# Expert passes of a two-block transformer kernel: gate tables from two-byte products with tokens innermost, 64 candidates for 256, all weight subtractions on VectorE

## Chip, cores and metric

The kernel runs on one core of a Trainium2 chip. The metric is the device time of one launch in microseconds (us); the median of three runs of the kernel before is 3660.84 us (3656.49 to 3661.97).

## What is computed

Two transformer blocks over 512 tokens, in float32. The change lies in the expert layer that ends the first block: 8 heads, each of which picks 16 of 16,384 one-neuron experts for each token through two lists of 128 keys.

```python
v1, i1 = lax.top_k(s1, PEER_TOPK)          # 16 of 128 keys, for each head and token
v2, i2 = lax.top_k(s2, PEER_TOPK)
cand = (v1[..., :, None] + v2[..., None, :]).reshape(PEER_CHUNK, PEER_HEADS, PEER_TOPK * PEER_TOPK)
sc, ci = lax.top_k(cand, PEER_TOPK)        # 16 of 256 sums
idx = (jnp.take_along_axis(i1, ci // PEER_TOPK, axis=-1) * PEER_N_KEYS
       + jnp.take_along_axis(i2, ci % PEER_TOPK, axis=-1))
g = jax.nn.softmax(sc, axis=-1)
act = jax.nn.gelu(jnp.einsum('chkd,cd->chk', peer_u[idx], hc), approximate=False) * g
return jnp.einsum('chk,chkd->cd', act, peer_v[idx])
```

## The kernel before

After attention and the state-space branch, the layer is worked in two passes over all experts, and for the first 128 tokens by gathers.

**Tokens 128 to 511, dense.** Pass 1 (`phase_p1`, with `experts_in` as its loop) takes 128 steps, one for each value of the second key. A step loads 512 KB of `peer_u`, splits it into a high part `whi` (ScalarE, L267) and the rest `wlo` (the subtraction of L268), and makes 24 matmuls of 384 columns into `pl` (lines 273 to 275: high by high, high by rest, rest by high). A Gelu writes `A`, and every second step a DMA writes `A` to memory (`adram`). The subtraction runs on VectorE (DVE in the profile) or, where `W.lo_eng` says so, on GpSimd (POOL): every second step of pass 1, about every third of pass 2.

**Gate tables.** `route(t)` works through tile t of 128 tokens on VectorE: the best 16 of each of 16 key lists (lines 1175 to 1179), 256 sums a head (L1186), the best 16 of these (lines 1193 to 1197), a softmax, and the two key numbers of each pick (lines 1216 to 1218, a compare, a product and a reduction of 2048 elements). For tiles 1 to 3 the picks are turned so that a token is a column, and for each block of 4 tokens (96 blocks in all) VectorE builds the one-hot tables `O`: for each token three instructions of 128 elements (lines 1251 to 1253), which take the token's key numbers and gate as one value per partition. Twelve matmuls of 128 columns (L1257) turn a block into its gate table in `pG`, ScalarE copies it to `G` (L1258), and after 8 blocks a DMA writes 2 MB to `gdram`.

**Tokens 0 to 127, sparse.** Once tile 0 is routed, 256 gathers by GpSimd (L1107) bring one row of `peer_u` or `peer_v` for each token and pick, 512 KB each, into a ring of 6; VectorE takes a dot product (L1116, 128 of them) or adds the row times its gate to `sacc` (L1126).

**Pass 2** (`phase_p2`) takes 128 steps over `peer_v`: `prep` multiplies `A` by its gate (L1289; for 8 steps at a time `fetch` reads back `A` and `G`), splits the product into `ahl` (lines 267, 268), and 18 matmuls of 512 columns go into six accumulators `acc`. After it come the second block's layers, which the change does not touch.

**What sets the order.** Each engine works its queue in order. The queue's order is fixed when the program is built, by a planner that replays the program on its own clock; the loop in `phase_p1` deals out routing and sparse work against a budget for each dense step (`have`, `some`), with the costs that stand behind `yield`. Buffers are rings by tag: `O` has 3, `A` 2, `Gst` (for `G` and for what is read back) 2.

Of the kernel before, what the change touches and what calls it, by code (L numbers as in the profile page):

```python
# [12 lines left out]
F32 = mybir.dt.float32  # L13
# [237 lines left out]
class Kernel:  # L251
# [809 lines left out]
    def phase_p1(self):  # L1061
        nc, pp = self.nc, self.pp

        ring = self.p0.tile([128, 4, D], F32, name="ring", tag="xres")
        more = pp.tile([128, 2, D], F32, name="ring2")
        self.ring = [ring[:, j] for j in range(4)] + [more[:, j] for j in range(2)]
        self.hs = pp.tile([128, D], F32, name="hs")
        nc.gpsimd.dma_start(out=self.hs, in_=self.hdram)
        self.iotab = pp.tile([128, 128], BF16, name="iotab")
        nc.vector.tensor_copy(self.iotab, self.iota)  # L1070
        self.query()
        first, rest, dense = self.route(0), chain(*(self.route(t) for t in range(1, TT))), self.experts_in()
        self.sparse = self.sparse_experts()

        have = 0.0
        for n, _ in enumerate(dense):
            have += 3.7
            while have > 0 and (d := next(first, None)) is not None:
                have -= d
            if have > 0:  # L1080
                self.some(1.0)
                have -= 1.15
                while have > 0 and (d := next(rest, None)) is not None:
                    have -= d
# [11 lines left out]
    def sparse_experts(self):  # L1096
# [4 lines left out]
        self.sacc = pp.tile([128, D], F32, name="sacc")  # L1101
# [17 lines left out]
        v.tensor_tensor(dots, dots, self.sgate, op=OP.mult)  # L1119
        for n in range(128, 256):  # L1120
            fetch(n + R - 1)
            r, w = self.ring[n % R], dots[:, n - 128:n - 127]
            if n == 128:
                v.tensor_scalar(self.sacc, r, w, None, op0=OP.mult)
            else:
                v.scalar_tensor_tensor(self.sacc, r, w, self.sacc, op0=OP.mult, op1=OP.add)  # L1126
            yield

    def query(self):
# [3 lines left out]
        for c in range(16):  # L1133
            if c < 3:
                q = self.q01[c]
            else:
                q = pp.tile([128, S], F32, name="qp", tag="A", bufs=2)
                nc.scalar.copy(q, next(self.xw))
# [6 lines left out]
    def experts_in(self):  # L1145
# [3 lines left out]
        for n in range(128):  # L1149
            self.W.lo_eng = nc.gpsimd if n % 2 else None  # L1150
# [5 lines left out]
            if n % 2 == 0:  # L1156
                A = pp.tile([128, 2, SD], F32, name="A", tag="A", bufs=2)
# [5 lines left out]
    def route(self, t):  # L1163
# [5 lines left out]
        io16 = self.iota[:, :16]  # L1169
        val = pp.tile([128, 16, 16], F32, name="val")  # L1170
        ix = pp.tile([128, 16, 16], U32, name="ix")
        for c in range(16):
            s = self.sall[t // 2][:, t % 2, c]
            w = pp.tile([128, 256], F32, name="w", bufs=1)
            v.max(val[:, c, :8], s)
            v.max_index(ix[:, c, :8], val[:, c, :8], s)
            v.match_replace(w[:, :128], val[:, c, :8], s, LOW)
            v.max(val[:, c, 8:], w[:, :128])
            v.max_index(ix[:, c, 8:], val[:, c, 8:], w[:, :128])
            yield 1.6  # L1180
        ixf = pp.tile([128, 8, 2, 16], BF16, name="ixf")
        v.tensor_copy(ixf.rearrange("p h i k -> p (h i) k"), ix)
        cand = pp.tile([128, 8, 16, 16], F32, name="cand", tag="cand")
        vv = val.rearrange("p (h i) k -> p h i k", i=2)
        sh = [128, 8, 16, 16]
        v.tensor_tensor(cand, vv[:, :, 0, :, None].to_broadcast(sh), vv[:, :, 1, None, :].to_broadcast(sh), op=OP.add)  # L1186
        yield 2.3
        sc = pp.tile([128, 8, 16], F32, name="sc")
        ci = pp.tile([128, 8, 16], U32, name="ci")
        for h in range(8):  # L1190
            s = cand[:, h].rearrange("p a b -> p (a b)")
            w = pp.tile([128, 256], F32, name="w", bufs=1)
# [5 lines left out]
            yield 2.3  # L1198
# [9 lines left out]
        k = pp.tile([128, 2, 8, 16], U32, name="k")  # L1208
        kf = pp.tile([128, 2, 8, 16], F32, name="kf")
        v.tensor_scalar(k[:, 0], ci, 4, None, op0=OP.logical_shift_right)  # L1210
        v.tensor_scalar(k[:, 1], ci, 15, None, op0=OP.bitwise_and)
        v.tensor_copy(kf, k)
        yield 1.5
        for i in range(2):
            eq = pp.tile([128, 8, 16, 16], BF16, name="eq", tag="cand")
            v.tensor_tensor(eq, kf[:, i, :, :, None].to_broadcast(sh), io16[:, None, None, :].to_broadcast(sh), op=OP.is_equal)
            v.tensor_tensor(eq, eq, ixf[:, :, i, None, :].to_broadcast(sh), op=OP.mult)
            v.tensor_reduce(r3[:, i], eq, axis=AX.X, op=OP.add)
            yield 5.5
# [18 lines left out]
        half = lambda x, h: x.bitcast(BF16).rearrange("p (n h) -> p n h", h=2)[:, :, h]
        v.tensor_copy(half(g3[:, 0], 1), half(T3[:, 2], 1))
        v.tensor_tensor(left, T3[:, 2], half(g3[:, 0], 1), op=OP.subtract)  # L1240
        v.tensor_copy(half(g3[:, 0], 0), half(left, 1))
        v.tensor_tensor(g3[:, 1], left, half(g3[:, 0], 0), op=OP.subtract)
        for b in range(0, 128, 4):
# [715 lines left out]
```

## Time and profile before

| | |
|---|---|
| median of 3 runs | 3660.84 us (3656.49 to 3661.97) |
| the profiled execution | 3660.37 us |
| its span | 3658.6 us |
| TensorE (PE) busy | 3309.3 us, 90% of the span |
| VectorE (DVE) busy | 2597.9 us, 71% |
| ScalarE (ACT) busy | 1325.2 us, 36% |
| GpSimd (POOL) busy | 1349.2 us, 37% |
| pass 1, first matmul of 384 columns to last gate table | about 586 to 1409 us |
| pass 2, first to last matmul into `acc` | 1438.0 to 2033.5 us |

Times in the trace count from the span's start. The shares are means over stages with different limits, so the stages are read one by one. Idle time carries the name of what ended it. "L268" is a line of the kernel; the subtractions of all weights have this one line.

### The profile page before, as it was taken

The page shows a single profiled execution, that of the slowest core. Times are in us where ns is not written, and L with a number is a line of the kernel's source. Part 1 is how long each engine was busy: PE and PEld are TensorE (multiplying, and loading weights), DVE is VectorE, ACT ScalarE, POOL GpSimd, SP SyncE. Part 2 cuts the span into 40 slices and gives each one's busy share as a digit, 9 for nine tenths or more (in the row PEclk, how much of TensorE's full clock was granted, in tenths as well). Part 3 has the DMA queues.
Part 4 walks back from the last instruction along what each step waited for, and adds up shares of the span by engine and source line. Part 5 has one row for each costly group of instructions (what it writes and reads, how often), then busy time and mean ns, then how long its engine had stood idle before and what let it go on. Part 6 is the DMA issues. An engine that isn't in the chain of part 4 may idle for free.

```text
span 3658.6 us, 47432 instructions
## 1 busy us (share of the span) xinstructions
PE 3309.3 (90%) x17407; PEld 2782.9 (76%) x17407; DVE 2597.9 (71%) x5062; ACT 1325.2 (36%) x2267; POOL 1349.2 (37%) x1284
## 2 busy tenths in 40 slices
PE   6877999889889785888999999999999999999998
PEld 5666789878777764666888887788888877888886
DVE  8999447999999998898555777455543686455533
ACT  4234433233233231223333366334431475334431
POOL 6577112662652643674122145431101245331101
PEclk9888999899989886999999999999999999999999
DMA  3222233975875866998665311322222311313322
GB/s 123 85 72 84 88 115 130 320 261 203 300 253 210 305 244 231 347 360 320 225 219 173 130 41 47 115 81 88 95 96 98 126 36 41 133 65 104 98 92 75
DMA packets 173867, 569.87 MB, mean 156 GB/s; under 512 B 18864, under 2 KB 52657, under 8 KB 167617
## 3 DMA queue, kind: packets, MB, share of 16 engines
q1 hardware_dynamic: 114576, 352.37, 28.6%
q0 software_dynamic: 40752, 157.30, 12.0%
q10 hardware_dynamic: 18304, 57.15, 4.1%
q8 instruction: 137, 2.24, 0.3%
q14 instruction: 98, 0.80, 0.1%
HBM read 503.33 MB, written 63.44 MB: 155 GB/s over the span
## 4 chain that ended last, share of the span: by engine, by line
PE 56%; DVE 28%; issue 7%; POOL 5%; DMA 2%; ACT 2%; SPq 0%; DVEq 0%; POOLq 0%; ACTq 0%
PE pl L273 7%; PE pl L274 7%; PE pl L275 7%; DVE ring L1116 4%; PE acc L274 4%; PE acc L275 4%; PE acc L273 3%; DVE wlo L268 2%; DVE O L1252 2%; PE mm L273 2%; PE mm L274 2%; PE mm L275 2%; DVE O L1253 2%; DVE O L1251 2%; DVE sacc L1126 1%
## 5 line engine op out<-in xcount | busy, mean ns | idle before, releaser
L267 ACT CAST whi<-wraw 128x1024 fp32r<-128x1024 f32 x523 | 544.7, 1047 | 950.4 <-PE pl L274 347.6
L268 DVE TENSOR_TENSOR wlo<-wraw,whi 128x1024 fp32r<-128x1024 f32 x352 | 448.0, 1273 | 522.5 <-ACT whi L267 508.3
L268 POOL TENSOR_TENSOR wlo<-wraw,whi 128x1024 fp32r<-128x1024 f32 x171 | 435.2, 2547 | 774.6 <-ACT whi L267 770.2
L275 PE MATMUL pl<-hhi,wlo 128*128 128x384 f32 (+1 forms) x1128 | 408.8, 365 | 64.3 <-POOL wlo L268 37.8
L273 PE MATMUL pl<-hhi,whi 128*128 128x384 f32 (+1 forms) x1128 | 407.9, 362 | 7.6 <-ACT whi L267 7.6
L274 PE MATMUL pl<-hlo,whi 128*128 128x384 f32 (+1 forms) x1128 | 404.6, 359 | 0.0
L274 PE MATMUL pl<-xTlo,whi 128*128 128x512 f32 x944 | 370.3, 392 | 0.0
L273 PE MATMUL pl<-xThi,whi 128*128 128x512 f32 x944 | 369.9, 392 | 0.0
L275 PE MATMUL pl<-xThi,wlo 128*128 128x512 f32 x944 | 367.4, 390 | 0.0
L274 PE MATMUL acc<-wlo,ahl 128*128 128x512 f32 x744 | 299.6, 403 | 21.6 <-DVE wlo L268 16.7
L273 PE MATMUL acc<-whi,ahl 128*128 128x512 f32 x744 | 254.7, 399 | 49.6 <-ACT ahl L267 28.8
L275 PE MATMUL acc<-whi,ahl 128*128 128x512 f32 x744 | 295.6, 400 | 0.0
L275 PEld LDWEIGHTS pl<-hhi,wlo 128*128 128x128 f32 x1128 | 225.1, 200 | 77.0 <-POOL wlo L268 41.9
L1107 POOL DMA_INDIRECT ring<-in_peer_v,sidx x128 | 180.6, 1411 | 199.1 <-DVE sacc L1126 136.1
L273 PEld LDWEIGHTS pl<-hhi,whi 128*128 128x128 f32 x1128 | 225.7, 200 | 18.9 <-ACT whi L267 10.2
L1107 POOL DMA_INDIRECT ring<-in_peer_r,sidx x128 | 169.3, 1323 | 165.4 <-DVE dots L1116 89.9
L274 PEld LDWEIGHTS pl<-hlo,whi 128*128 128x128 f32 x1128 | 225.1, 200 | 4.1
L1940 POOL TENSOR_TENSOR cv<-cv 128x512 f32<-128x512 f32 x44 | 57.1, 1297 | 430.7 <-ACT cv L1939 430.7
L273 PEld LDWEIGHTS acc<-whi,ahl 128*128 128x128 f32 x744 | 139.9, 189 | 88.5 <-ACT ahl L267 29.1
L273 PEld LDWEIGHTS pl<-xThi,whi 128*128 128x128 f32 x944 | 177.2, 188 | 39.0 <-issue 0.5
L275 PEld LDWEIGHTS pl<-xThi,wlo 128*128 128x128 f32 x944 | 177.2, 188 | 38.7 <-issue 0.5
L274 PEld LDWEIGHTS pl<-xTlo,whi 128*128 128x128 f32 x944 | 177.3, 188 | 36.7 <-issue 1.0
(698 smaller groups left out, 7937.5 us busy)
## 6 DMA issues: line engine op xcount, KB each, us to landing
wraw<-in_peer_u SPq DMA_DIRECT2D x128, 512.0 KB
wraw<-in_peer_v SPq DMA_DIRECT2D x128, 512.0 KB
wraw<-in_up SPq DMA_DIRECT2D x88, 512.0 KB
adram<-A ACTq DMA_DIRECT2D x64, 384.0 KB
A<-adram SPq DMA_DIRECT2D x16, 1536.0 KB
gdram<-G ACTq DMA_DIRECT2D x12, 2048.0 KB
G<-gdram SPq DMA_DIRECT2D x16, 1536.0 KB
wraw<-in_down SPq DMA_DIRECT2D x44, 512.0 KB
```

What stands on the lines that cost most here:

```text
L267: self.nc.scalar.copy(hi, src)
L268: (eng or self.nc.vector).tensor_tensor(lo, src, hi.bitcast(F32), op=OP.subtract)
L273: mm(out, l[0], r[0], start=start, stop=False)
L274: mm(out, l[0], r[1], start=False, stop=False)
L275: mm(out, l[1], r[0], start=False, stop=stop)
L1107: nc.gpsimd.indirect_dma_start(out=self.ring[n % R], out_offset=None, in_=src[n // 128], in_offset=bass.IndirectOffsetOnAxis(ap=self.sidx[ ...
L1116: v.tensor_tensor_reduce(r, r, self.hs, 1.0, 0.0, op0=OP.mult, op1=OP.add, accum_out=dots[:, n:n + 1])
L1126: v.scalar_tensor_tensor(self.sacc, r, w, self.sacc, op0=OP.mult, op1=OP.add)
L1251: v.tensor_scalar(O[:, 0, j], self.iotab, i1, None, op0=OP.is_equal)
L1252: v.tensor_scalar(Ow[:, j], self.iota, i2, ga, op0=OP.is_equal, op1=OP.mult)
L1253: v.tensor_scalar(O[:, 3, j], self.iotab, i2, gb, op0=OP.is_equal, op1=OP.mult)
L1940: nc.gpsimd.tensor_tensor(ts[0], ts[0], ts[1], op=OP.mult)
```

## The change

Five things are done. A block's tables `O` are built by two instructions in place of twelve: one compare of 1024 elements and one product of 1536, all in two-byte floats, with the four tokens innermost; a gate is held as three two-byte terms. Of the 256 sums only the 64 that can hold a best 16 are formed, in four pieces, and the place of a pick is worked back from its position by some small instructions; the two key numbers are picked by two-byte products and a tree of additions, ScalarE spreading the key numbers out. All subtractions of weights in both passes go to VectorE. The budget of `phase_p1` is changed. The first read-back is a method of its own, called from the end of pass 1 if routing is done. Ring sizes: `O` 2 for 3, `A` 3 for 2.

```diff
         for n, _ in enumerate(dense):
-            have += 3.7
+            have += 3.85
...
-                self.some(1.0)
-                have -= 1.15
...
+                self.some(1.1)
+                have -= 1.3
...
+            if n >= 122 and not left and not self.AG:
+                self.fetch_ag(0)
...
         for n in range(128):
-            self.W.lo_eng = nc.gpsimd if n % 2 else None
             w = self.W.next()
...
-        cand = pp.tile([128, 8, 16, 16], F32, name="cand", tag="cand")
+        cand = pp.tile([128, 8, 64], F32, name="cand", tag="sums")
...
+        for a, na, nb in ((0, 1, 16), (1, 3, 8), (4, 4, 4), (8, 8, 1)):
...
+        nc.scalar.copy(ei[:, 1], ix.rearrange("p (h i) k -> p h i k", i=2)[:, :, 0, :, None].to_broadcast([128, 8, 16, 16]))
...
-            eq = pp.tile([128, 8, 16, 16], BF16, name="eq", tag="cand")
-            v.tensor_tensor(eq, kf[:, i, :, :, None].to_broadcast(sh), io16[:, None, None, :].to_broadcast(sh), op=OP.is_equal)
-            v.tensor_tensor(eq, eq, ixf[:, :, i, None, :].to_broadcast(sh), op=OP.mult)
-            v.tensor_reduce(r3[:, i], eq, axis=AX.X, op=OP.add)
...
+            v.tensor_tensor(e, self.iota16[:, None].to_broadcast(sh), kb[:, i, :, None, :].to_broadcast(sh), op=OP.is_equal)
+            v.tensor_tensor(e, e, ei[:, 1], op=OP.mult)
...
+            for m in (8, 4, 2):
+                v.tensor_tensor(e[:, :, :m], e[:, :, :m], e[:, :, m:2 * m], op=OP.add)
+            v.tensor_tensor(r3[:, i], e[:, :, 0], e[:, :, 1], op=OP.add)
...
-            O = pp.tile([128, 4, 4, 128], BF16, name="O", tag="O", bufs=3)
-            Ow = O[:, 1:3].rearrange("p e j i -> p (e j i)").bitcast(F32).rearrange("p (j i) -> p j i", j=4)
-            for j in range(4):
-                i1, i2, ga, gb = (x[:, b + j:b + j + 1] for x in (T3[:, 0], T3[:, 1], g3[:, 0], g3[:, 1]))
-                v.tensor_scalar(O[:, 0, j], self.iotab, i1, None, op0=OP.is_equal)
-                v.tensor_scalar(Ow[:, j], self.iota, i2, ga, op0=OP.is_equal, op1=OP.mult)
-                v.tensor_scalar(O[:, 3, j], self.iotab, i2, gb, op0=OP.is_equal, op1=OP.mult)
+            O = pp.tile([128, 5, 128, 4], BF16, name="O", tag="O", bufs=2)
+            s2, s3 = [128, 2, 128, 4], [128, 3, 128, 4]
+            v.tensor_tensor(O[:, :2], self.iota4[:, None].to_broadcast(s2), T3[:, :, None, b:b + 4].to_broadcast(s2), op=OP.is_equal)
+            v.tensor_tensor(O[:, 2:], O[:, 1:2].to_broadcast(s3), g3[:, :, None, b:b + 4].to_broadcast(s3), op=OP.mult)
             pg = self.bank("o", [128, 4, 128], "pG")
             for j in range(4):
-                for k, m in enumerate((half(Ow[:, j], 1), half(Ow[:, j], 0), O[:, 3, j])):
-                    nc.tensor.matmul(pg[:, j], O[:, 0, j], m, start=k == 0, stop=k == 2)
+                for k in range(3):
+                    nc.tensor.matmul(pg[:, j], O[:, 0, :, j], O[:, 2 + k, :, j], start=k == 0, stop=k == 2)
...
-            self.W.lo_eng = nc.gpsimd if n % 3 == 2 or n == 125 else None
             ws.append((n, self.W.next(held=0)) + act.pop(n))
             if n < 116:
-                self.some(1.22)
+                self.some(1.2)
```

The planner's order moves at two places that matter here. On VectorE, late in pass 1 where gate tables are built (`O` are the tables, one number for each block; `T3` and `g3` hold key numbers and gates, `wlo` is a weight subtraction, `sacc` a sparse step), the queue before held:

```order
L1252 TENSOR_SCALAR O_12495<-pack1_70,T3_11557,g3_11559 128x128
L1253 TENSOR_SCALAR O_12495<-iotab_4227,T3_11557,g3_11559 128x128
L1251 TENSOR_SCALAR O_12522<-iotab_4227,T3_11557 128x128
L1252 TENSOR_SCALAR O_12522<-pack1_70,T3_11557,g3_11559 128x128
L1253 TENSOR_SCALAR O_12522<-iotab_4227,T3_11557,g3_11559 128x128
```

Three instructions stand there for each token. On the same engine, at a like place, the queue now holds:

```order
L1286 TENSOR_TENSOR O_11108<-iota4_4227,T3_10348 128x1024
L1286 TENSOR_TENSOR O_11125<-iota4_4227,T3_10348 128x1024
L268 TENSOR_TENSOR wlo_11527<-wraw_11338,whi_11526 128x1024
L1135 SCALAR_TENSOR_TENSOR sacc_11788<-ring2_4224,dots_5384,sacc_11788 128x1024
L1287 TENSOR_TENSOR O_11108<-O_11108,g3_10349 128x1536
L1287 TENSOR_TENSOR O_11125<-O_11125,g3_10349 128x1536
L268 TENSOR_TENSOR wlo_11580<-wraw_11390,whi_11579 128x1024
```

Two instructions stand for a block of four tokens where twelve stood, with sparse steps and subtractions between them. Counted over the whole queue, ahead of the last table stand 221 of the 256 sparse steps where 154 stood, and 163 weight subtractions where 98 stood. In GpSimd's queue no subtraction is left between the first and the last gather.

On SyncE, whose queue loads weights (`wraw`) and reads back `A` and `G` (here `G2`), the seam of the two passes was:

```order
L224 DMA wraw_11489<-in_peer_u 128x1024
L224 DMA wraw_11522<-in_peer_v 128x1024
L224 DMA wraw_11624<-in_peer_v 128x1024
L224 DMA wraw_11686<-in_peer_v 128x1024
L224 DMA wraw_11775<-in_peer_v 128x1024
L224 DMA wraw_11837<-in_peer_v 128x1024
L224 DMA wraw_12607<-in_peer_v 128x1024
L1275 DMA G2_12588<-gdram_81 128x12x256
L1275 DMA G2_12596<-gdram_81 128x12x256
```

On SyncE the seam is now:

```order
L224 DMA wraw_11530<-in_peer_u 128x1024
L224 DMA wraw_11583<-in_peer_v 128x1024
L224 DMA wraw_11622<-in_peer_v 128x1024
L224 DMA wraw_11657<-in_peer_v 128x1024
L224 DMA wraw_11692<-in_peer_v 128x1024
L224 DMA wraw_11727<-in_peer_v 128x1024
L224 DMA wraw_11784<-in_peer_v 128x1024
L1303 DMA G2_11615<-gdram_81 128x12x256
L1303 DMA G2_11773<-gdram_81 128x12x256
```

The first read of `G` stands where it stood, behind the last load of `peer_u` and six loads of `peer_v`.

## Rows read from the trace of the kernel before

**Rows 1.** Busy time by stretch: PE, PEld, DVE, ACT, POOL; clock, DMA share, GB/s.

```profile
586.00:1410.00 824.00, 703.44 (x4205) 634.91 (x4204) 811.64 (x2223) 253.53 (x370) 373.28 (x225) 0.89 0.70 247
1410.00:1438.00 28.00, 0.00 (x0) 0.00 (x0) 13.93 (x14) 0.55 (x2) 12.29 (x10) 0.50 1.00 365
1438.00:1740.00 302.00, 259.61 (x1054) 201.49 (x1055) 261.10 (x267) 85.87 (x117) 183.78 (x117) 0.97 0.92 339
1740.00:2033.00 293.00, 293.00 (x1265) 236.41 (x1265) 165.79 (x187) 102.92 (x141) 67.50 (x42) 1.00 0.58 197
```

**Rows 2.** Waits of PE, 586 to 1439 us: total, times, longest.

```profile
PE pG L1257 <- DVE O L1252: 38.4, 91, 4.3
PE pl L275 <- POOL wlo L268: 37.8, 13, 7.2
PE acc L273 <- ACT ahl L267: 28.8, 1, 28.8
PE pl L275 <- DVE wlo L268: 26.4, 10, 6.1
```

**Rows 3.** Groups by form on DVE, 497 to 1410 us: busy us, mean ns.

```profile
L1116 DVE CUSTOM_DVE_ANT_0 ring<-ring,hs 128x1024 f32<-128x1024 f32 x128 | 186.7, 1475 | 7.0 <-DMA ring<-in_peer_r,sidx 6.9
L1252 DVE TENSOR_SCALAR O<-pack,T,g 128x128 f32<-128x128 f32 x384 | 153.5, 405 | 0.0
L1253 DVE TENSOR_SCALAR O<-iotab,T,g 128x128 bf16<-128x128 bf16 x384 | 129.2, 342 | 0.0
L1251 DVE TENSOR_SCALAR O<-iotab,T 128x128 bf16<-128x128 bf16 x384 | 110.5, 296 | 0.1
L268 DVE TENSOR_TENSOR wlo<-wraw,whi 128x1024 fp32r<-128x1024 f32 x78 | 104.1, 1335 | 26.6 <-ACT whi L267 26.5
...
L1216 DVE TENSOR_TENSOR eq<-kf,pack 128x2048 bf16<-128x2048 f32 x8 | 18.2, 2275 | 0.0
L1218 DVE TENSOR_REDUCE r<-eq 128x128 f32<-128x2048 bf16 x8 | 18.2, 2273 | 0.0
...
L1179 DVE FIND_INDEX8 ix<-val,w 128x8 uint32<-128x128 f32 x64 | 18.2, 284 | 0.0
...
L1197 DVE FIND_INDEX8 ci<-sc,w 128x8 uint32<-128x256 f32 x32 | 13.3, 417 | 0.0
```

**Rows 4.** Single lines on DVE: shortest, median and longest ns; first and last start.

```profile
L1251 DVE TENSOR_SCALAR O<-iotab,T x384: 224/242/3150, 776.3 to 1408.2; 128x128 bf16<-128x128 bf16 x192
L1252 DVE TENSOR_SCALAR O<-pack,T,g x384: 327/333/3197, 784.6 to 1408.3; 128x128 f32<-128x128 f32 x192
L1253 DVE TENSOR_SCALAR O<-iotab,T,g x384: 293/302/3145, 787.0 to 1408.6; 128x128 bf16<-128x128 bf16 x192
L1116 DVE CUSTOM_DVE_ANT_0 ring<-ring,hs x128: 1194/1214/3937, 647.0 to 1241.8; 128x1024 f32<-128x1024 f32 x128
L1126 DVE SCALAR_TENSOR_TENSOR sacc<-ring,dots,sacc x127: 1228/1280/3957, 1249.0 to 1698.2; 128x1024 f32<-128x1024 f32 x127
L268 DVE TENSOR_TENSOR wlo<-wraw,whi x64: 1196/1210/3741, 591.3 to 1408.8; 128x1024 fp32r<-128x1024 f32 x64
L1217 DVE TENSOR_TENSOR eq<-eq,ixf x8: 1209/1212/3383, 626.7 to 1284.8; 128x2048 bf16<-128x2048 bf16 x8
```

**Rows 5.** Timeline at 999 us: start, length, engine, instruction.

```profile
999.44 3.94 DVE L1116 CUSTOM_DVE_ANT_0 ring<-ring,hs 128x1024 f32<-128x1024 f32 x1
...
999.87 2.41 POOL L268 TENSOR_TENSOR wlo<-wraw,whi 128x1024 fp32r<-128x1024 f32 x1
```

**Rows 6.** Timeline of DVE at 1402 us: one token's three table instructions, and the next token.

```profile
1402.40 0.24 DVE L1251 TENSOR_SCALAR O<-iotab,T 128x128 bf16<-128x128 bf16 x1
...
1403.04 0.24 DVE L1251 TENSOR_SCALAR O<-iotab,T 128x128 bf16<-128x128 bf16 x1
```

**Rows 7.** Timeline of DVE at the seam of the passes.

```profile
1436.85 0.56 DVE L1289 TENSOR_TENSOR A<-A,G 128x384 f32<-128x384 f32 x1 [10.45 <-DMA G<-gdram]
```

**Rows 8.** The page's group of the first 128 gathers on POOL: busy us, mean ns.

```profile
L1107 POOL DMA_INDIRECT ring<-in_peer_r,sidx x128 | 169.3, 1323 | 165.4 <-DVE dots L1116 89.9
```

More of the change, by code (lines that the diff above doesn't have):

```diff
@@ L1075, in phase_p1 @@
         have = 0.0
+        left = True
         for n, _ in enumerate(dense):
-            have += 3.7
+            have += 3.85
             while have > 0 and (d := next(first, None)) is not None:
@@ L1080, in phase_p1 @@
             if have > 0:
-                self.some(1.0)
-                have -= 1.15
-                while have > 0 and (d := next(rest, None)) is not None:
-                    have -= d
+                self.some(1.1)
+                have -= 1.3
+                while have > 0 and left:
+                    d = next(rest, None)
+                    left = d is not None
+                    have -= d or 0.0
                 have = min(have, 0.0)
+            if n >= 122 and not left and not self.AG:
+                self.fetch_ag(0)
         for _ in chain(first, rest):
@@ L1119, in sparse_experts @@
         v.tensor_tensor(dots, dots, self.sgate, op=OP.mult)
+        self.sacc = pp.tile([128, D], F32, name="sacc", tag="hs")
         for n in range(128, 256):
@@ L1136, in query @@
             else:
-                q = pp.tile([128, S], F32, name="qp", tag="A", bufs=2)
+                q = pp.tile([128, S], F32, name="qp", tag="A", bufs=3)
                 nc.scalar.copy(q, next(self.xw))
@@ L1190, in route @@
         for h in range(8):
[L1191 to L1192 removed]
+            s = cand[:, h]
+            w = pp.tile([128, 128], F32, name="w", bufs=1)[:, :64]
             v.max(sc[:, h, :8], s)
@@ new lines, in route @@
+        kf = pp.tile([128, 3, 8, 16], F32, name="kf")
+        v.tensor_scalar(k[:, 0], ci, 3, None, op0=OP.logical_shift_right)
+        v.tensor_scalar(k[:, 1], ci, 2, None, op0=OP.logical_shift_right)
+        v.tensor_copy(k[:, 2], ci)
+        v.tensor_copy(kf, k)
+        a, b, p = kf[:, 0], kf[:, 1], kf[:, 2]
+        v.tensor_scalar(a, a, 1.0, 0.0, op0=OP.subtract, op1=OP.max)
+        v.scalar_tensor_tensor(a, b, 6.0, a, op0=OP.subtract, op1=OP.max)
+        v.scalar_tensor_tensor(a, p, 48.0, a, op0=OP.subtract, op1=OP.max)
@@ new lines, in route @@
+        yield 2.5
+        kb = pp.tile([128, 2, 8, 16], BF16, name="kb")
+        v.tensor_copy(kb[:, 0], a)
+        st = pp.tile([128, 8, 16], F32, name="st")
+        v.tensor_scalar(st, a, 48.0, None, op0=OP.add)
+        for m, q in ((4.0, 24.0), (8.0, 8.0)):
+            v.tensor_scalar(b, a, m, q, op0=OP.mult, op1=OP.add)
+            v.tensor_tensor(st, st, b, op=OP.min)
+        v.scalar_tensor_tensor(st, a, 16.0, st, op0=OP.mult, op1=OP.min)
+        v.tensor_tensor(kb[:, 1], p, st, op=OP.subtract)
@@ L1232, in route @@
             nc.tensor.transpose(pT[:, i], r3[:, i].rearrange("p h k -> p (h k)"), self.ident)
-        T3 = pp.tile([128, 3, 128], F32, name="T3")
-        nc.scalar.copy(T3, pT)
-        g3 = pp.tile([128, 2, 128], F32, name="g3", bufs=2)
+        T3 = pp.tile([128, 2, 128], BF16, name="T3", bufs=2)
+        g3 = pp.tile([128, 3, 128], BF16, name="g3", bufs=2)
         left = pp.tile([128, 128], F32, name="left")
[L1238 to L1242, printed above, removed]
+        nc.scalar.copy(T3, pT[:, :2])
+        nc.scalar.copy(left, pT[:, 2])
+        for i in range(3):
+            v.tensor_copy(g3[:, i], left)
+            if i < 2:
+                v.tensor_tensor(left, left, g3[:, i], op=OP.subtract)
+        yield 1.0
         for b in range(0, 128, 4):
@@ L1260, in route, with fetch_ag @@
                 nc.scalar.dma_start(out=self.gdram[(t - 1) * 4 + b // 32], in_=G)
-            yield 1.6
+            yield 1.55
+    def fetch_ag(self, g):
+        nc, pp = self.nc, self.pp
+        A = pp.tile([128, 8, SD], F32, name="A2", tag="A2", bufs=2)
+        G = pp.tile([128, SD // 32, 8, 32], F32, name="G2", tag="Gst", bufs=2)
+        nc.sync.dma_start(out=A, in_=self.adram[g])
+        nc.sync.dma_start(out=G, in_=self.gdram[:, :, g * 8:g * 8 + 8].rearrange("t p i k -> p t i k"))
+        self.AG[g] = (A, G)
     def phase_p2(self):
@@ L1296, in norm @@
             nc.gpsimd.dma_start(out=self.xdram[:, t], in_=self.xres[:, t])
-        fetch(0)
+        if not self.AG:
+            self.fetch_ag(0)
         prep(0)
```

62 lines of the change are left out of this document (30 added, 32 removed).

## The prediction

> **What bounds the kernel now.** I read the busy time by stretch first, since the shares of the whole span hide the stages [rows 1]. From 586 to 1410 us, pass 1, VectorE is busy 811.6 of 824 us and TensorE 703.4: pass 1 ends when VectorE has done its queue. The waits agree: TensorE waits there for tables and for subtractions, on VectorE and on GpSimd alike [rows 2]. From 1410 to 1438 us TensorE does nothing: the last table must be written, read back (VectorE sits 10.45 us until `G` has landed [rows 7]) and multiplied, and one wait of 28.8 us stands for it [rows 2]. From 1438 to 1740 us TensorE and VectorE are both busy about 86%, and the DMA engines 92%. From 1740 us TensorE is busy without a gap, 1265 matmuls in 293 us, 0.232 us each [rows 1]; the 2304 matmuls of pass 2 would take 534 us at that pace and take 595.5 (1438.0 to 2033.5). So there are two things to win: VectorE's work before the last table, and some 60 us of stalls in pass 2.
>
> Then VectorE's groups [rows 3] against the median of the same lines [rows 4]. Most longest cases are about 2 to 3 us over the median, and one pair shows why: a dot product takes 3.94 us instead of 1.21 while a subtraction of 2.41 us runs on GpSimd [rows 5]. Mean less median, times count: 21 + 28 + 15 us for the three table lines, 33 for the dot products, 10 for the subtractions on VectorE: 107 us that VectorE spends held up.
>
> **The change part by part.** The sum is VectorE's time up to the last table. An instruction's price is its median less 0.08 us, since the next one starts before it ends: one token's three instructions last 877 ns by their medians [rows 4] and the next token starts 0.64 us after [rows 6].
>
> Gate tables: 96 blocks at 4 x 0.64 = 2.56 us now. The new instructions have two tensor inputs of two bytes; the one like them is the product of 2048 elements, 1212 ns [rows 4], where the compare with a float32 input takes 2275 [rows 3]. Two searches of 128 and 256 elements, 284 and 417 ns [rows 3], give 1.04 ns an element and 0.15 us fixed, so the product streams at 0.52 ns. Then 1024 elements take 0.68 and 1536 take 0.95 us, less 0.16: 1.47 us a block, 96 x 1.09 = **105 us less**. Bounds: 1.35 us a block, if the product's whole 1212 ns scale with 2560 elements and all of 0.16 is saved, and 2.8 if they stream at 1.04 ns; I take the product's own pace, the nearest row.
>
> Subtractions: the held-up 107 us go, since no subtraction is left on GpSimd: **107 less** (between 64, the table lines alone, and 120). For it VectorE has 65 more of its own ahead of the last table, at 1.13 us: **73 more**.
>
> Sparse steps: 67 more ahead of the last table, at 1.20 us (line 1126) [rows 4]: **80 more**, taken from pass 2.
>
> Best 16 of 64: five operations a head lose 192 elements each, 1.0 us by the slope, 32 us over 32 heads; short dependent operations may not gain all of it, so **21 less** (13 to 32).
>
> The picks and the rest: two of the three steps of a pick fall from about 2.27 us [rows 3] to 1.21 and to four additions of together about 1.6; the sums shrink; some 14 small instructions a tile, of about 0.25 us, are added: **5 less** (15 less to 15 more).
>
> Sum: -105 - 107 + 73 + 80 - 21 - 5 = **-85 us**, so 727 us of work where 811.6 were. Idle time was 12 us; I add 20, because `O` has two buffers for three (VectorE now waits for TensorE's matmuls of the block before the last), TensorE and DMA come closer to their limits, and sparse rows must arrive faster (bounds 0 and 60). The last table then comes at about 1345 instead of 1410 us, 65 earlier.
>
> What lies beside: TensorE's own 703 us [rows 1] fit into the 759 us from 586 to 1345, so 56 us of cover are left; its table matmuls now read with a step of 4 elements, which no row shows, and 50 ns more on each of 1152 would use that cover up. ScalarE gets 8 copies of 2048 elements, some 2 us each as an estimate from VectorE's 2275 ns for as many; it is busy 253 of 824 us, and a weight split queued behind one is covered by the two weights split ahead.
>
> The seam: SyncE's queue has the first read of `G` where it was, and tables still come last, so the 28 us stay and the early call counts nothing (bounds 0 and 28 less). First matmul of pass 2: 1438 - 65 = 1373 us.
>
> Pass 2: only some 23 sparse steps are left for it, and no subtraction blocks VectorE. VectorE's 165.8 of 293 us after 1740 [rows 1] grow by a third of 70 subtractions, 27 us, and TensorE's gapless 293 us cover that. I take 534 us and 16 for the start: **550, 45 less** (20 to 57).
>
> In all -65 - 45 = -110 us, against the profiled execution's 3660.4 us, which is as good as the median 3660.8: **3550 us**.
>
> [...] The change makes all tables two-input instructions and puts more gathers beside them; what gathers would do, if they blocked as subtractions do, is the last rival.
>
> **The rivals.** *VectorE waits for rows and buffers.* Pass 1 moved 247 GB/s x 824 us = 204 MB at a DMA share of 0.70; 67 gathers of 0.52 MB make it 239 MB, and in 759 us that is 315 GB/s, a share of 0.89. In the one stretch with such a share, 0.92, VectorE was busy only 86% [rows 1]. At 92% its 727 us take 790: last table 1376, first matmul 1404, total 3581. At 86% they take 845 and pass 1 gains nothing: 3636. For it: three engines near their limits. Against: the only wait of the dot products for data was 6.9 us [rows 3]. I price it at 3590.
>
> *Everything falls well.* No added idle time, 32 us from the 64 candidates, pass 2 at 534 us: -85 - 11 - 61 = -157, 3503. For it: 12 us of idle time in 824 now.
>
> *Products at one element a tick, the other side.* If a stream in runs of four elements, with one input repeated, does not run at the product's pace, a block costs 2.8 us, 23 more instead of 105 less, and the two-byte instructions of the picks add some 20: the sum is +63, with 20 idle the last table comes 83 later, and with 45 won in pass 2 the time is 3698. It decides from 2.6 us a block, where 110 us are used up. Against: the 1212 ns are of a product with one input repeated in runs of 16. That would also be the change not doing what it says.
>
> *Gathers as blockers, also the other side.* 128 gathers took 169 us of GpSimd, 1.32 us each [rows 8]. If each of the 221 gathers in pass 1 held VectorE for that, it would lose 290 us, 3840. Against: 154 sparse steps already ran there beside tables, and the 107 us held up are used up by 64 subtractions at about 1.7 us each.
>
> **How the numbers follow.** Forecast 0.60, the likeliest, its own range 3515 to 3580; waits 0.20; all well 0.11; products slow 0.06; gathers 0.03. The range leaves out the slow products, the gathers, the worst third of the waits and a little below: 3500 to 3605. About 0.2%, 7 us, is what a measurement of this kernel can tell from no change. Faster by more: the first three cases, 0.91; within it 0.02, from weak forms of the two slow ones; slower 0.07.
>
> **What would show it.** Right: lines 1286 and 1287 at about 0.68 and 0.95 us; no dot product or `sacc` step beyond 1.5 us; the last table near 1345 us with VectorE busy about 95% from 586 us; some 28 us without a matmul before `acc`; pass 2 in 550 us with TensorE over 95% busy. Wrong: table instructions at 1.2 and 1.75 us; sparse steps still held for 2 us beside gathers; VectorE under 90% in pass 1, waiting for `ring` rows, for `pG` or for `whi`; table matmuls so slow that TensorE sets pass 1's end; or `acc` still waiting for subtractions in pass 2.

## The result, and the profile after

The changed kernel takes 3529.69 us (median of 4 runs, 3527.84 to 3532.42) against 3659.40 (3656.49 to 3661.97) for the kernel before, measured beside it: a ratio of 0.9646 [0.963, 0.9663], 129.7 us less. The forecast was 110 less, 3550, with a range of 3500 to 3605.

Busy time of the changed kernel by stretch (columns as in [rows 1]): pass 1 up to the last table, the seam, and pass 2 in two parts.

```profile
586.00:1330.50 744.50, 693.04 (x4191) 668.97 (x4190) 687.64 (x1472) 266.86 (x376) 342.68 (x228) 0.95 0.87 320
1330.50:1362.20 31.70, 0.52 (x5) 0.23 (x2) 15.34 (x15) 1.13 (x3) 13.57 (x12) 0.50 1.03 378
1362.20:1600.00 237.80, 229.07 (x988) 188.00 (x989) 154.50 (x203) 80.36 (x111) 29.71 (x29) 0.98 0.75 263
1600.00:1901.00 301.00, 301.00 (x1334) 248.85 (x1332) 163.40 (x225) 107.33 (x147) 7.12 (x21) 1.00 0.59 202
```

Against [rows 1]: the last table stands at 1331 us instead of 1409 (78 earlier), the seam, in which TensorE waits, is 31.2 us instead of 28.8 (2 longer), and pass 2 takes 538.8 us (1362.2 to 1901.0) instead of 595.5 (57 shorter). Before rounding the sum is 132.5, the difference of the two spans, 3658.6 and 3526.1. VectorE was busy all but 12 us of pass 1 before; now it is idle for 57 of 744.5, and TensorE for only 51. The bound has moved.

Waits of TensorE from 586 to 1400 us in the changed kernel: total, times, longest.

```profile
PE acc L273 <- ACT ahl L267: 31.2, 1, 31.2
PE pl L275 <- DVE wlo L268: 23.5, 17, 4.2
PE pl L273 <- ACT whi L267: 15.6, 12, 3.3
PE pG L1291 <- DVE O L1287: 12.1, 7, 2.9
```

The 37.8 us for subtractions on GpSimd [rows 2] are gone, and the wait for tables has fallen from 38.4 to 12.1. VectorE's groups from 586 us up to the last table of the changed kernel, busy us and mean ns as in [rows 3]:

```profile
L268 DVE TENSOR_TENSOR wlo<-wraw,whi 128x1024 fp32r<-128x1024 f32 x127 | 154.0, 1213 | 4.5 <-ACT whi L267 4.4
L1124 DVE CUSTOM_DVE_ANT_0 ring<-ring,hs 128x1024 f32<-128x1024 f32 x128 | 153.9, 1211 | 4.2 <-DMA ring<-in_peer_r,sidx 4.2
L1135 DVE SCALAR_TENSOR_TENSOR sacc<-ring,dots,sacc 128x1024 f32<-128x1024 f32 x94 | 120.1, 1278 | 0.1
L1287 DVE TENSOR_TENSOR O<-O,g 128x1536 bf16<-128x1536 bf16 x96 | 89.3, 947 | 0.1
L1286 DVE TENSOR_TENSOR O<-iota,T 128x1024 bf16<-128x1024 bf16 x96 | 65.2, 686 | 43.7 <-PE pG L1291 43.7
...
L1246 DVE TENSOR_TENSOR ei<-iota,kb 128x2048 bf16<-128x2048 bf16 x8 | 9.7, 1214 | 0.0
L1247 DVE TENSOR_TENSOR ei<-ei 128x2048 bf16<-128x2048 bf16 x8 | 9.7, 1213 | 0.0
L1209 DVE MAX8 sc<-w 128x8 f32<-128x64 f32 x32 | 7.1, 222 | 0.4
```

Three things are to be seen. The table instructions last 0.69 and 0.95 us. Every mean is now near its median: dot products 1211 ns where they had 1475 [rows 3]. And VectorE waits 43.7 us, 37 times, for the table matmuls to free one of the two `O` buffers. These matmuls are the surprise, since they take twice as long as before. A bunch of 24 on TensorE in the changed kernel, between two matmuls of pass 1:

```profile
1202.19 0.34 PE L274 MATMUL pl<-hlo,whi 128*128 128x384 f32 x1
1202.37 3.01 PE L1291 MATMUL pG<-O 128*128 128x128 bf16 x24
1205.13 0.43 PE L275 MATMUL pl<-hhi,wlo 128*128 128x384 f32 x1
```

24 matmuls in 2.76 us are 115 ns each. In the kernel before, the same number took 1.35 us up to the start of the next matmul, 56 ns each:

```profile
906.29 1.54 PE L1257 MATMUL pG<-O 128*128 128x128 bf16 x24
907.64 0.42 PE L273 MATMUL pl<-hhi,whi 128*128 128x384 f32 x1
```

They now read their operands with a step of four two-byte elements, 8 bytes. By these bunches 1152 times 59 ns, some 68 us, are an estimate of what the step costs TensorE; e6 below measures it. TensorE's busy time from 586 us to the last table fell all the same, from 703.4 to 693.0 us: before, the table matmuls came largely three at a time, token by token, between those of pass 1, and kept TensorE busy for 143.4 us; now they come in twelves and more and take 147.0.

The seam of the changed kernel (start, length, engine, instruction): the last table is written, the reads of `G` go out 9.5 us after, and VectorE can start 20 us after that.

```profile
1331.67 0.33 ACTq L1294 DMA_DIRECT2D gdram<-G  x1
...
1341.19 24.10 SPq L1303 DMA_DIRECT2D G<-gdram  x3
...
1361.06 3.84 DVE L1323 TENSOR_TENSOR A<-A,G 128x384 f32<-128x384 f32 x8 [9.97 <-DMA G<-gdram]
```

Meanwhile 12 gathers run, and the DMA engines are full (share 1.03).

### The profile page after: what moved, and what is told of

It is laid out like the page before. It is cut to its first block, busy times and chain, and to the rows that moved or that the text cites. A ratio compares the mean times of both kernels' runs of the same rounds, so it can differ in the third digit from the quotient of the medians.

```text
span 3526.1 us, 46554 instructions
## 1 busy us (share of the span) xinstructions
PE 3277.6 (93%) x17407; PEld 2816.4 (80%) x17407; DVE 2368.7 (67%) x4292; ACT 1340.0 (38%) x2278; POOL 1102.2 (31%) x1178
## 4 chain that ended last, share of the span: by engine, by line
PE 73%; DVE 17%; POOL 4%; issue 3%; ACT 2%; DMA 2%; SPq 0%; DVEq 0%; ACTq 0%; POOLq 0%
PE pl L273 10%; PE pl L275 10%; PE pl L274 10%; PE acc L274 5%; PE acc L275 5%; PE acc L273 5%; PE pG L1291 3%; PE mm L273 2%; PE mm L274 2%; PE mm L275 2%; DVE ring L1124 2%; DVE wlo L268 2%; PE T L274 2%; PE T L275 2%; PE T L273 1%
## 5 line engine op out<-in xcount | busy, mean ns | idle before, releaser
L268 DVE TENSOR_TENSOR wlo<-wraw,whi 128x1024 fp32r<-128x1024 f32 x457 | 560.6, 1228 | 653.0 <-ACT whi L267 639.2
L275 PE MATMUL pl<-hhi,wlo 128*128 128x384 f32 (+1 forms) x1128 | 394.0, 351 | 23.6 <-DVE wlo L268 23.5
L273 PE MATMUL pl<-hhi,whi 128*128 128x384 f32 (+1 forms) x1128 | 395.9, 351 | 15.6 <-ACT whi L267 15.6
L274 PE MATMUL pl<-hlo,whi 128*128 128x384 f32 (+1 forms) x1128 | 391.5, 347 | 0.0
L273 PE MATMUL acc<-whi,ahl 128*128 128x512 f32 x744 | 278.4, 392 | 35.8 <-ACT ahl L267 31.2
L274 PE MATMUL acc<-wlo,ahl 128*128 128x512 f32 x744 | 291.8, 392 | 4.1 <-DVE wlo L268 4.1
L275 PE MATMUL acc<-whi,ahl 128*128 128x512 f32 x744 | 289.2, 391 | 0.0
L1115 POOL DMA_INDIRECT ring<-in_peer_r,sidx x128 | 177.9, 1390 | 328.9 <-DVE w L1184 157.7
L1115 POOL DMA_INDIRECT ring<-in_peer_v,sidx x128 | 201.7, 1575 | 230.4 <-DVE sacc L1135 147.7
L275 PEld LDWEIGHTS pl<-hhi,wlo 128*128 128x128 f32 x1128 | 217.9, 193 | 34.1 <-DVE wlo L268 30.1
L268 POOL TENSOR_TENSOR wlo<-wraw,whi 128x1024 fp32r<-128x1024 f32 x66 | 163.9, 2488 | 252.5 <-ACT whi L267 252.2
```

The lines of the kernel that those rows point to most:

```text
L268: (eng or self.nc.vector).tensor_tensor(lo, src, hi.bitcast(F32), op=OP.subtract)
L273: mm(out, l[0], r[0], start=start, stop=False)
L274: mm(out, l[0], r[1], start=False, stop=False)
L275: mm(out, l[1], r[0], start=False, stop=stop)
L1115: nc.gpsimd.indirect_dma_start(out=self.ring[n % R], out_offset=None, in_=src[n // 128], in_offset=bass.IndirectOffsetOnAxis(ap=self.sidx[ ...
```

## The experiments

My theory after the result: the change frees VectorE as forecast, but its layout makes table matmuls twice as long, so TensorE now sets the end of pass 1. The rivals stand in the expectations. Twelve kernels ran, in three batches, each beside runs of the kernel before (medians 3657.2, 3657.4 and 3654.8 us). Differences are given against the changed kernel's 3529.7 unless another is named; between batches they are good to about 5 us. Line numbers move by a few from kernel to kernel; the names of the tiles do not.

**e1: subtractions on GpSimd again**

```diff
+            self.W.lo_eng = nc.gpsimd if n % 2 else None
...
+            self.W.lo_eng = nc.gpsimd if n % 3 == 2 or n == 125 else None
```

> The changed kernel with one part undone: GpSimd does every second weight subtraction of pass 1 and every third of pass 2 again. Theory (a subtraction on GpSimd holds VectorE for longer than VectorE would need for it): VectorE saves 64 x 1.14 = 73 us of its own in pass 1 and is held for about 107 us, the dot products reach 3 to 4 us again, the last gate table comes 20 to 40 us later and the time is 3550 to 3570 us. Rival (the gain came from the tables alone, and handing work to GpSimd would help): VectorE is free 70 us earlier and the time is 3470 to 3515 us.

3592.68 us (3588.92 to 3595.72), 63 more: the theory's direction, but above its range, and the last table came 38 us earlier (1292) and not later. VectorE's groups of this kernel, 497 to 1400 us, and behind them GpSimd's:

```profile
L1124 DVE CUSTOM_DVE_ANT_0 ring<-ring,hs 128x1024 f32<-128x1024 f32 x128 | 176.3, 1385 | 2.6 <-DMA ring<-in_peer_r,sidx 2.6
L1135 DVE SCALAR_TENSOR_TENSOR sacc<-ring,dots,sacc 128x1024 f32<-128x1024 f32 x88 | 129.9, 1477 | 7.8 <-DMA ring<-in_peer_v,sidx 6.4
L1288 DVE TENSOR_TENSOR O<-O,g 128x1536 bf16<-128x1536 bf16 x96 | 112.1, 1179 | 0.2
L268 DVE TENSOR_TENSOR wlo<-wraw,whi 128x1024 fp32r<-128x1024 f32 x75 | 111.1, 1482 | 44.3 <-ACT whi L267 44.3
L1287 DVE TENSOR_TENSOR O<-iota,T 128x1024 bf16<-128x1024 bf16 x96 | 81.7, 858 | 30.7 <-PE pG L1292 27.9 <-issue 2.8
...
L268 POOL TENSOR_TENSOR wlo<-wraw,whi 128x1024 fp32r<-128x1024 f32 x62 | 163.6, 2640 | 162.7 <-ACT whi L267 131.3 <-issue 30.6
```

Mean less the changed kernel's mean, times count: 22 + 18 + 22 + 20 + 17 = 99 us that VectorE is held up by 62 subtractions, 1.6 us each, where doing one itself costs 1.13. That is the loss on VectorE; how it becomes 63 us of time is not so clear, since the order moved too. Only 54 sparse additions stand ahead of the last table where 93 stood, and the planner put matmuls of pass 1 behind it: they ran until the first `acc`, which came at 1407 us, 45 later, without a seam before it. Pass 2, with 15 us of waits for GpSimd, took 558, 19 longer. b1 is the cleaner test.

**b1: the kernel before, with that one part**

```diff
-            self.W.lo_eng = nc.gpsimd if n % 2 else None
-            self.W.lo_eng = nc.gpsimd if n % 3 == 2 or n == 125 else None
```

> Edit: the kernel before with one thing of the change alone, all subtractions of weights on VectorE. Theory (a subtraction on GpSimd holds VectorE as long as doing it there would): no dot product over 1.6 us is left, the last table comes 20 to 50 us earlier than in the kernel before, pass 2 gains some 15 to 40, total 3585 to 3635. Rival (VectorE sets the end of pass 1, and 64 more subtractions of 1.2 us lengthen its queue): 3655 to 3720.

3618.07 us (3615.39 to 3622.44), ratio 0.9892 [0.9872, 0.9912]: the theory. No dot product lasted over 1.30 us and no table instruction over 0.57, where the longest had taken 3.94 and 3.20 [rows 4], the last table came 27 us earlier (1382), and pass 2 took 580 us, 15 less.

**e7: the twelve-instruction tables again** (all else as changed, two `O` buffers)

```diff
-            v.tensor_tensor(O[:, :2], self.iota4[:, None].to_broadcast(s2), T3[:, :, None, b:b + 4].to_broadcast(s2), op=OP.is_equal)
-            v.tensor_tensor(O[:, 2:], O[:, 1:2].to_broadcast(s3), g3[:, :, None, b:b + 4].to_broadcast(s3), op=OP.mult)
...
+            for j in range(4):
...
+                v.tensor_scalar(O[:, 0, j], self.iotab, i1, None, op0=OP.is_equal)
...
```

> The changed kernel with the gate tables of before: twelve instructions of 128 elements for a block of four tokens, token values as one value per partition, all else as changed, two buffers of O. Theory (the tables took 2.56 us a block and take 1.47): 96 x 1.09 = 105 us more on VectorE in pass 1, of which TensorE's matmuls on contiguous tables give back up to 37 us: 3600 to 3635 us. Rival (VectorE has slack in pass 1 now, TensorE sets its end): below 3560 us.

3591.23 us (3584.77 to 3597.8), 62 more: between the two. VectorE is the bound again, and the stretch to its last table reads:

```profile
586.00:1376.60 790.60, 684.72 (x4183) 618.82 (x4181) 766.34 (x2401) 263.60 (x372) 286.90 (x208) 0.89 0.80 289
```

VectorE is busy 766.3 of 790.6 us, 79 more than with the new tables, although 20 fewer sparse additions stand ahead of its last table (73 for 93). The table comes only 46 us later, since VectorE is idle for 24 us and no longer for 57: its wait for `pG` is 4.2 us, the table matmuls being quick again (their records, which overlap, last 229 ns in the median, 297 in the changed kernel). Pass 2 is 14 us longer.

**e5: tokens outermost**

```diff
-            v.tensor_tensor(O[:, :2], self.iota4[:, None].to_broadcast(s2), T3[:, :, None, b:b + 4].to_broadcast(s2), op=OP.is_equal)
...
+            v.tensor_tensor(O[:, :2], self.iotab[:, None, None].to_broadcast(s2), T3[:, :, b:b + 4, None].to_broadcast(s2), op=OP.is_equal)
...
```

> The changed kernel with the tokens outermost: O is 5 x 4 x 128, so the compare and the product read one token's value repeated along the innermost 128 elements, and the table matmuls read contiguous columns. Theory (two elements a tick need an innermost run of distinct neighbours on both inputs): the two table instructions take about 1.22 and 1.75 us in place of 0.69 and 0.95, 128 us more in pass 1, some 37 us given back by TensorE: 3610 to 3660 us. Rival (the pace does not depend on the innermost step): the table instructions stay at 0.69 and 0.95 us, the matmuls get cheaper and the time is 3490 to 3530 us.

3643.82 us (3641.71 to 3646.15), 114 more: the theory. Single lines on VectorE in this kernel (shortest, median, longest ns):

```profile
L1286 DVE TENSOR_TENSOR O<-iotab,T x96: 1205/1220/1234, 753.7 to 1467.3; 128x1024 bf16<-128x1024 bf16 x96
L1287 DVE TENSOR_TENSOR O<-O,g x96: 1733/1754/1769, 767.3 to 1468.6; 128x1536 bf16<-128x1536 bf16 x96
```

The same elements and types take 1.78 and 1.85 times as long when one input is a value repeated along the innermost axis. This was the rival of slow products, real in the other layout. In this kernel no gather was left for the seam, and it took 16 us; e8 came from that.

**e6: tables as two pairs of tokens**

```diff
-            O = pp.tile([128, 5, 128, 4], BF16, name="O", tag="O", bufs=2)
+            O = pp.tile([128, 5, 2, 128, 2], BF16, name="O", tag="O", bufs=2)
...
-                    nc.tensor.matmul(pg[:, j], O[:, 0, :, j], O[:, 2 + k, :, j], start=k == 0, stop=k == 2)
+                    nc.tensor.matmul(pg[:, j], O[:, 0, j // 2, :, j % 2], O[:, 2 + k, j // 2, :, j % 2], start=k == 0, stop=k == 2)
```

> Edit: the tables of a block are stored as two pairs of tokens, so that a table matmul reads its operands with a step of 4 bytes instead of 8; everything else as in the changed kernel. Theory (the step in bytes slows TensorE's reads, and TensorE is what pass 1 now runs against): the table matmuls in a bunch fall from 115 ns each to 83 to 100, TensorE's busy time before the last table falls by 15 to 35 us, part of it comes back as waits, total 3505 to 3522. Rival 1 (any step other than one element costs the same): 115 ns stay, total 3526 to 3534. Rival 2 (VectorE's streams of two elements no longer run at two elements a tick): the two table instructions take 1.2 and 1.75 us instead of 0.69 and 0.95, total 3570 to 3650.

3483.36 us (3480.39 to 3485.32), ratio 0.9523 [0.9505, 0.9541], 46 less: more than the theory's range allowed. VectorE's instructions keep 0.69 and 0.95 us. A bunch on TensorE in this kernel:

```profile
794.72 1.55 PE L1294 MATMUL pG<-O 128*128 128x128 bf16 x24
796.08 0.42 PE L275 MATMUL pl<-hhi,wlo 128*128 128x384 f32 x1
```

And its stretch to the last table (columns as in [rows 1]):

```profile
586.00:1286.00 700.00, 628.47 (x4186) 602.61 (x4185) 683.32 (x1467) 263.80 (x376) 377.30 (x228) 0.97 0.91 340
```

With a step of 4 bytes a table matmul takes 57 ns, about as before the change; with 8 bytes, 115. (In e5, where the elements lie side by side, 24 took 1.33 us, 55 ns each.) TensorE is busy 628.5 us where it was 693.0, 64.5 less, VectorE's wait for `pG` falls from 43.7 us to 4.0, and the last table comes 45 us earlier (1286). Both operands of a table matmul changed their step together; which of the two slows it was not tried.

**e4: three `O` buffers** (two for `A`; the index tile `k` shares the buffer of the 64 sums)

```diff
-            O = pp.tile([128, 5, 128, 4], BF16, name="O", tag="O", bufs=2)
+            O = pp.tile([128, 5, 128, 4], BF16, name="O", tag="O", bufs=3)
...
-            tag = ("O", 2) if 0 <= n - (128 - self.LAST) < self.LAST - 3 else ("A", 3)
+            tag = ("A", 2) if 0 <= n - (128 - self.LAST) < self.LAST - 3 else ("O", 3)
...
```

> The changed kernel with three buffers of O and two of A, as before the change (the index tile k shares the space of the 64 sums). Theory (the 43.7 us in which VectorE waits for the table matmuls come from having two buffers): most of them go, the last table comes 20 to 40 us earlier, 3490 to 3512 us. Rival (TensorE is as busy as VectorE in pass 1, so the wait turns up at another place): 3520 to 3535 us.

3530.62 us (3528.89 to 3532.43): no change, as the rival has it, but not for its reason. The last table does come 14 us earlier (1317), VectorE's wait for `pG` falls to 30.1 us, and pass 2 takes 550.2 us, 11 longer. Matmuls into `acc` alone, in a gapless stretch of the changed kernel, and then of this one (busy us of PE, count):

```profile
1650.00:1900.00 250.00, 249.18 (x1096) 205.34 (x1095) 2.65 (x4) 1.00 0.58 197
```

```profile
1650.00:1899.00 249.00, 247.99 (x1063) 199.04 (x1062) 2.65 (x4) 1.00 0.57 192
```

That is 227 ns a matmul against 233, at the same granted clock of 1.00; 2304 of them make 14 us. In the four kernels whose gated `ahl` lies in the ring of three `O` buffers (before, b1, e4, e12) it is 233, in the others, where it lies in the ring of `A`, 226 to 228. What in the place decides is open. Three buffers for both were not tried.

**e8: gathers held back in the seam**

```diff
-                self.some(1.1)
+                self.some(1.8)
...
         prep(0)
+        z = pp.tile([128, 1], F32, name="z0")
+        v.tensor_scalar(z, self.AG[0][0][:, 0, :1], 0.0, None, op0=OP.mult)
...
+        v.tensor_scalar(rows, rows, z, None, op0=OP.add)
+        held = pp.tile([128, 128], U32, name="sidx2")
+        v.tensor_copy(held, rows)
+        self.sidx = held
```

> Edit: the row numbers that the gathers of pass 2 use depend on the first gated A (zero times it is added), so that no more than the gathers already dealt to pass 1 can run between the last gate table and the first matmul of pass 2; pass 1's rate of sparse steps is set to 1.8 for 1.1 so that about as many steps (87 for 105 in the order) stand ahead of the last table. Theory (the gathers share the DMA engines with the read of G and lengthen it): the stretch without matmuls falls from 31.5 us to 16 to 23, total 3513 to 3522. Rival (write and read of G take that long by themselves): 28 to 32 us stay, total 3526 to 3536.

3520.20 us (3511.58 to 3524.53), 9 less: the theory. Nine is not much beside the 5 us between batches; that the seam is shorter is read from the trace. The seam of this kernel:

```profile
1330.62 0.33 ACTq L1294 DMA_DIRECT2D gdram<-G  x1
1336.92 12.30 SPq L1303 DMA_DIRECT2D G<-gdram  x3
1344.99 3.85 DVE L1323 TENSOR_TENSOR A<-A,G 128x384 f32<-128x384 f32 x8 [16.66 <-DMA G<-gdram]
```

The write takes 6.3 us instead of 9.5, the read 8.1 instead of 19.9, and TensorE waits 16.2 us instead of 31.2. Pass 2 gives 9 of it back (547.5 us); it has 18 more sparse additions.

**e10: as e8, with 46 sparse additions ahead of the last table instead of 87**

```diff
-                self.some(1.8)
+                self.some(1.45)
```

> Edit: as the one before, but with a rate of 1.45, which leaves 46 sparse additions ahead of the last table instead of 87. Theory (TensorE, not VectorE, is now what pass 1 runs against: it is busy 693 of 744 us): taking some 50 us off VectorE's queue moves the last table by no more than 15 us against the run before, and pass 2 stays within 10 us, total within 12 us of that run. Rival (VectorE's queue still sets the last table): it comes 30 to 50 us earlier, and the total falls by 20 us or more.

3539.97 us (3535.37 to 3542.27), 20 more than e8. 41 additions, some 49 us of VectorE's time, bring the last table only 13 us forward (1317), as the theory says; that pass 2 would stay within 10 us and the total within 12 was wrong. Pass 2 took 578.0, 30 longer, its first part at a DMA share of 0.95:

```profile
1333.00:1600.00 267.00, 228.66 (x944) 180.15 (x945) 221.68 (x260) 77.71 (x107) 115.17 (x94) 0.96 0.95 356
```

**e14: 256 candidates again**

```diff
-        cand = pp.tile([128, 8, 64], F32, name="cand", tag="sums")
+        cand = pp.tile([128, 8, 256], F32, name="cand", tag="cand")
...
```

> Edit: the changed kernel with 256 sums a head again instead of 64 (the five search operations at 256 wide, the position split by a shift and a mask). Theory (TensorE sets the end of pass 1 in the changed kernel, so VectorE's time there is largely covered): VectorE has 25 to 35 us more to do, the total rises by only 5 to 18 us, 3534 to 3548. Rival (VectorE's queue sets it, as the sum of the prediction has it): 3550 to 3566.

3544.40 us (3541.64 to 3548.01), 15 more: the theory. VectorE was busy 42 us longer before the last table, which came 26 us later, and pass 2 was 12 shorter. Part of this is order: 107 sparse additions stand ahead of the table for 93 (the 105 that the expectation of e8 names is counted to the first matmul of pass 2).

This kernel also shows what the step of 8 bytes does. From 1274 us to the last table TensorE does little but table matmuls, with gaps between them, at a granted clock of 0.50. A bunch of 12 at 1.00, one at 0.50, and the second's stretch:

```profile
971.11 1.59 PE L1276 MATMUL pG<-O 128*128 128x128 bf16 x12
1286.52 1.58 PE L1276 MATMUL pG<-O 128*128 128x128 bf16 x12 [1.09 <-DVE O L1272]
1280.00:1300.00 20.00, 12.23 (x95) 4.69 (x8) 0.50 0.77 254
```

They take equally long, whereas 12 with contiguous tables take 0.84 us at 1.00 and 1.46 at 0.50 in e5. So with this step the granted clock does not set the pace of a table matmul.

**e11, e12, e13: towards the best version.** e11 joins e6 and e8; e12 adds the buffers of e4; e13 is e11 with a higher rate:

```diff
-                self.some(1.8)
+                self.some(2.1)
```

> Edit: tables as pairs of tokens and the held gathers together (rate 1.8, 87 sparse additions ahead of the last table). Theory (the two gains lie in different stretches and add): about 45 us earlier last table, a stretch without matmuls of 16 us instead of 31, pass 2 some 8 us longer for 18 more sparse steps in it, total 3468 to 3480. Rival (what the held gathers give at the seam is paid back in pass 2): 3481 to 3490.

3471.64 us (3468.36 to 3478.02), ratio 0.9502 [0.9478, 0.9526]: the gains add, and this is the fastest version, 58 us under the changed kernel. Last table 1277, seam 16, pass 2 547.5 us. Stretch to the last table:

```profile
586.00:1276.50 690.50, 625.18 (x4168) 599.75 (x4167) 672.80 (x1437) 262.37 (x373) 355.47 (x216) 0.97 0.90 336
```

VectorE, busy 672.8 of 690.5 us, is again what pass 1 runs against.

> Edit: as the one before, with three buffers for the tables O instead of two (and two for A instead of three). Theory (once the table matmuls are quick, VectorE waits for them only 4 us in all, so a third buffer has nothing to give): within 6 us of the run before. Rival (the 17 us that TensorE waits for tables come from bursts that a third buffer evens out): 8 to 17 us less.

3474.70 us (3472.2 to 3479.89), the same within the spread, but again as a sum of two: last table 9 us earlier, seam 2 longer, pass 2 14 longer with `ahl` in the `O` ring.

> Edit: as the pair and hold kernel, with a rate of 2.1, so that 108 instead of 87 sparse additions stand ahead of the last table. Theory (with quick table matmuls VectorE is again about as full as TensorE in pass 1): the last table comes 10 to 25 us later, pass 2 is 8 to 16 us shorter, total within 8 us of the pair and hold kernel. Rival (pass 1 has room for them, as TensorE sets its end): the last table moves by under 8 us, total 8 to 16 us less.

3491.79 us (3485.75 to 3493.94), 20 more than e11; neither. The last table moved 16 us later and pass 2 became 14 shorter, as the theory says, but the additions dealt to pass 1 were late and their gathers ran in the seam again. TensorE's wait there:

```profile
PE acc L273 <- ACT ahl L267: 32.2, 1, 32.2
```

## Why the prediction was right

The forecast, -110, lay 20 us from the -130 measured; the likeliest case happened, some of its terms offset each other, and one of its named unknowns turned out badly without showing in the total, which was luck. Most of its signs came: tables at 0.69 and 0.95 us, no held-up sparse step, pass 2 in 539 us with TensorE busy 98% of it. VectorE was busy 92% of pass 1 and not 95%, and one of its signs of being wrong came as well: TensorE now sets the end of pass 1.

- **Gate tables, 105 less on VectorE: right.** 0.69 and 0.95 us less 0.16 are 1.48 us a block; the forecast had 1.47. e5 shows what it hung on: the tokens innermost.
- **Held-up time, 107 less: right, somewhat small.** No sparse step is over 1.29 us. e1 brings 99 us back with 62 subtractions. Lines not counted had been held up too: the 26 sparse additions of pass 1 took 1522 ns in the mean for a median of 1280.
- **Subtractions on VectorE ahead of the last table, 127 for 64 [rows 4], and sparse additions, 94 for 26: right.** They cost 71 and 82 us; the forecast had 73 and 80.
- **Best 16 of 64, 21 less: too small.** The five operations take 222, 218, 209, 221 and 211 ns, 0.99 us a head under the old ones (one of them in [rows 3], 417 ns), so 32 us in 32 heads, the top of the range.
- **Picks and the rest, 5 less: too small.** What remains of the measured 124 us (811.6 to 687.6) is about 33, of which the pick steps give some 18.
- **Idle time, 20 more: too small, and not for the reason first named.** It is 45 more, 43.7 of it for `pG`. The two `O` buffers alone do not make it: with two buffers and quick matmuls e6 waits 4.0 us, with three and slow ones e4 still 30.1. So the last table came 78 us earlier and not 65: 39 more work gone than forecast, 25 more idle.
- **TensorE's cover, 56 us, to be used up by 50 ns on each table matmul: the unknown came in at 59 ns.** It did not cost what it says, because TensorE's busy time did not rise by 68 us but fell by 10. The table matmuls had kept it busy for 143.4 us before, and the same matmuls of pass 1 into `pl` took 569.4 us instead of 625.6 (the two overlap); the prediction had priced neither. Matmuls into `pl` up to the last of them, in the kernel before, the changed one and e7 (busy us of PE first, then PEld, DVE and ACT; granted clock third from the end):

```profile
586.00:1338.00 752.00, 625.55 (x3041) 560.94 (x3042) 0.00 (x0) 61.93 (x127) 0.93 0.74 258
586.00:1312.40 726.40, 569.43 (x3032) 541.63 (x3030) 0.00 (x0) 61.99 (x126) 0.96 0.87 321
586.00:1260.00 674.00, 594.98 (x3022) 540.97 (x3020) 0.00 (x0) 61.48 (x126) 0.95 0.83 304
```

The mean granted clock (a mix of the two levels that the traces show, 0.50 and 1.00) is a part of this at most: e7, with the old tables in between, has nearly the changed kernel's clock and 26 us more. How much is clock and how much the bunching of the tables is open. Still, TensorE became the limit, and this is where the gain stopped: e6 takes the 59 ns away, and 46 us come back.

- **Seam 0, early read 0: nearly right.** The seam is 2 us longer. The first read of `G` stands in the queue where it stood; no run leaves the early call out, so that it does nothing is not shown by itself. What lengthens the seam, e8 shows: 12 gathers beside the write and the read of `G`.
- **Pass 2, 45 less: right, 11 small.** The floor of 534 us was the old pace, 0.232 us a matmul (0.233 without gaps); the new one is 0.227, so some 14 us of the 57 come with the new place of `ahl`, an edit costed at nothing (seen over all kernels, not tried by itself). The rest, 43, is near the forecast.

The rivals: gathers do not hold VectorE. They take 1.39 and 1.58 us on the page of the changed kernel, and a dot product beside one lasts what it always lasts:

```profile
998.92 1.21 DVE L1124 CUSTOM_DVE_ANT_0 ring<-ring,hs 128x1024 f32<-128x1024 f32 x1
999.00 1.95 POOL L1115 DMA_INDIRECT ring<-in_peer_v,sidx  x1 [4.06 <-DVE dots L1124]
```

Each subtraction on GpSimd costs VectorE some 1.6 us in e1; for the issue of gathers the trace shows no such loss, and of the 128 dot products none lasts over 1.27 us. Waits for rows came to 4.2 us for the dot products, at the DMA share of 0.87 that the rival expected to choke on.

## What to carry to other kernels

When one engine's work is laid out anew, price the readers on the other engines too: the layout that ran VectorE at 0.5 ns an element made TensorE read with a step of 8 bytes at half pace (115 ns a table matmul for 56), and pairs (4 bytes, 57 ns) kept both. Work given to an engine off the path can hold up the busy one for longer than the busy one would need to do it (in e1 some 1.6 us for 1.13), which is read from means above medians. And the length of a stretch between two passes depends on what else moves there (here 31.2 us with 12 gathers, 16.2 in e8 with none).

## What the runs showed that was not expected

- Table matmuls of 128 columns: 55 to 57 ns with operand steps of 2 and 4 bytes, 115 ns with 8, all at a granted clock of 1.00; at 0.50 a bunch with 8 bytes takes no longer, a contiguous one 1.46 us for 0.84.
- Two-byte products of 1536 elements: 0.95 us with inner runs of four or of two values (runs of two were open before e6); 1.75 us with one value repeated along the innermost axis, as e5's theory had it.
- Accumulating matmuls of 512 columns, gapless at a granted clock of 1.00: 227 or 233 ns by the ring in which their `ahl` lies; the cause is open.
